# A two-layer decoder trunk: layer 0's heads in pairs, their buffers in the residual's place, and another order of its column groups

## The chip, the cores and the metric

The kernel runs on one core of a Trainium2 chip. The metric is device time in microseconds. Three runs of the kernel before took 2193.85, 2195.46 and 2195.37 us, median 2195.37.

## The reference

x is 256 tokens of 2048 features, float32. Layer 0 mixes by two recurrences that share one input projection; layer 1 by dilated attention. Each layer ends in a squared-ReLU MLP.

```
proj = rms_norm(x) @ w_in
x_lru, y_lru, q_h, f_h, v_h, g_h = split(proj)
# RG-LRU: conv of width 4, block-diagonal gates, scan
xb = causal_depthwise_conv(x_lru);  r, i = sigmoid(xb @ w_a + b_a), sigmoid(xb @ w_i + b_i)
h_t = a_t * h_(t-1) + sqrt(1 - a_t^2) * i_t * xb_t,   a = exp(-8 r softplus(-lambda))
lru = h * gelu(y_lru)
# HGRN2, per head of 128: S_t = diag(f_t) S_(t-1) + k_t v_t,  o_t = q_t S_t
q = silu(q_h);  f = lb + (1 - lb) sigmoid(f_h);  k = (1 - lb) sigmoid(-f_h)
hg = rms_norm_per_head(o) * g_norm * silu(g_h)
x = x + concat(lru, hg) @ w_out
x = x + relu(rms_norm(x) @ w1)^2 @ w2
# layer 1: qkv, partial rotary, attention over three dilated windows, w_o, MLP; then a final RMSNorm
```

## The kernel before

Weights come in units of 128 x 2048 (1 MB). SP's queue loads a unit into one of three `raw` buffers (L148); ACT rounds it to `hi` (L130) and DVE takes the difference `lo` (L131), again in three buffers each, so that the split of a unit can begin when the unit three before it has been used. `tokens` multiplies two blocks of 128 tokens by four units: 24 matmuls of 512 columns a unit (hi x hi, hi x lo, lo x hi; L221), into two of the three PSUM banks called `p`. `tokens_group` evicts the two banks on ACT into a tile `tk` (L360).

Layer 0's input projection runs through 12 groups of 512 columns in the order of `ORDER`: v, q, f and g are the four parts of HGRN2, x and y those of the RG-LRU, 0 and 1 their halves; G0 and G1 stand for the block-diagonal gates (`lru_gates`: 48 matmuls of 256 columns each). While a group's units run, `HOOKS` hands out other work, one list after each unit. A scheduler that simulates the engines decides the final order of each engine's instructions within that; the engines then run their instructions in this order.

The hooked work is:

- `hgrn(hd)`, one call a head: the head's columns of q and f are transposed on PE into the bank `pt` (`turned`, L436); sigmoids on ACT; the decayed scores are built from the diagonal (`pd`, L457) and eight levels c = 1, 2, 4 to 128. In a level PE multiplies into `pl` (L473), the result goes into `st` by a masked copy on DVE (L476) or by ACT copies (L481, L483), and DVE multiplies the factors of the next level into `qk` (L490) and shortens `tot` (L492). Level c = 128 is L468, L469. The next level's matmuls need the multiply. Then the output products into `po` (L497 to L499) and their squares on ACT (L504).
- `finish(g, half)`: for two heads, norm and gate on DVE (L518, L520), transposes into `pt`, and the split into `bufb` blocks 8 to 15 (L271, L272). It needs the column group g.
- `lru_in(n, half)`: transposes and convolution (L535, L537), split into `bufb` blocks 0 to 7 (L268, L269); `lru_gates(n)`; `lru_gelu(n)` (needs y); `lru_out(n, half)`: transposes of y, product with the scan (L579), split into the same blocks.

`bufb` then holds the 16 blocks that `out_project` multiplies by `w_out`: two column groups by `tokens`, with the residual add into `xres`, and two by `second`, in a form with fewer products, whose first bank is `po`. `xres` is the tile `xall` seen by tokens; it is loaded from `xtok` at the start (L367, L379) for the first norm, and added to only after `w_out`. In `w_out`'s first eight rows `PAIRED` puts blocks 0, 2, 4, 6 into one unit and 1, 3, 5, 7 into the next. The units of one column group come in the order 2, 3, 0, 1, so HGRN2's rows come first.

Of the kernel before, what the change touches and what calls it, by code (L numbers as in the profile page):

```python
# [10 lines left out]
F32 = mybir.dt.float32  # L11
# [4 lines left out]
AF = mybir.ActivationFunctionType  # L16
OP = mybir.AluOpType
# [3 lines left out]
P = 128  # L21
S = 256
# [19 lines left out]
def trunk_kernel(ctx, tc, head, x, xtok, cols, tab, masks, pos, fin, w_in, w_gate, w_out, w_qkv, w_o, w1, w2, out):  # L42
    nc = tc.nc
# [8 lines left out]
    pmm = pool("pmm", 3, space=PSUM)  # L52
    psc = pool("psc", 1, space=PSUM)
# [30 lines left out]
    units = []  # L84
# [12 lines left out]
    for g, step in enumerate(ORDER.split()):  # L97
        if step[0] == "G":
            units.append((w_gate, int(step[1])))
        else:  # L100
            units.extend((w_in, 4 * PLACE[step] + i) for i in range(4))
    units.extend((w_out, 4 * n + g) for n in range(2) for g in (2, 3, 0, 1))
    plan2(w_out, 8)
    for layer in range(2):
        if layer:
# [8 lines left out]
    at = [0, 0]  # L114
# [111 lines left out]
    later, turns, steps = [], [], []  # L226
# [24 lines left out]
    def lut(out_, in_, func, **kw):  # L251
        i = A.activation(out_, in_, func, **kw)
        if luts["kind"] != tables[func]:
            luts.update(kind=tables[func], before=luts["now"], now=[])
        luts["now"].append(after(i, luts["now"][:1] or luts["before"]))

    def direct(p, w, jobs):
        p = p[:, :S]
# [173 lines left out]
    def turned(tiles, at):  # L432
        p = psc.tile([P, 2, S], F32, name="pt", bufs=1)
        for i, (z, m) in enumerate(zip(tiles, at)):
            for j in range(2):
                T.transpose(p[:, i, j * P:j * P + P], z[:, j, m * P:m * P + P], ident)  # L436
        return p

    def halves(t, c, second):
        return t.rearrange("p (n two c) -> p n two c", two=2, c=c)[:, :, int(second), :]  # L440

    def hgrn(hd):
        g, at = divmod(hd, 4)
        oml = omlb[:, hd:hd + 1]
        qk = wk.tile([P, 2 * S], F32, name="qk", bufs=3)
        qp, kq = qk[:, :S], qk[:, S:]
        p = turned((done[f"q{g}"], done[f"f{g}"]), (at, at))
        lut(qp, p[:, 0], AF.Sigmoid)
        V.scalar_tensor_tensor(qp, p[:, 0], oml, qp, op0=OP.mult, op1=OP.mult)
        f = wk.tile([P, S], F32, name="f", bufs=3)  # L450
        lut(f, p[:, 1], AF.Sigmoid)
        lut(kq, p[:, 1], AF.Sigmoid, scale=-1.0)
        A.activation(f, f, AF.Identity, scale=oml, bias=lb[:, hd:hd + 1])
        pd = psc.tile([P, 2, P], F32, name="pd", bufs=1)
        for j in range(2):
            js = slice(j * P, j * P + P)
            T.matmul(pd[:, j], kq[:, js], qp[:, js], start=True, stop=True)  # L457
        st = wk.tile([P, 3, P], F32, name="st", bufs=3)
        V.tensor_tensor(st[:, :2], pd, ident[:, None, :].to_broadcast([P, 2, P]), OP.mult)
        stf = st[:, :2].rearrange("p a b -> p (a b)")  # L460
        V.tensor_tensor(qp, qp, f, OP.mult)
        c = 1
        tot = f
        while c <= 128:
            pl = psc.tile([P, 2, 64], F32, name="pl", bufs=2)
            if c == 128:
                plf = pl.rearrange("p j c -> p (j c)")
                T.matmul(plf, kq[:, :P], qp[:, P:], start=True, stop=True)  # L468
                A.copy(st[:, 2], plf)  # L469
                break  # L470
            for j in range(2):
                js = slice(j * P, j * P + P)
                T.matmul(pl[:, j], kq[:, js], halves(qp[:, js], c, True), start=True, stop=True)  # L473
            if c <= 16:
                lv = LEVELS.index(c)
                V.copy_predicated(halves(stf, c, True), msk[:, lv].rearrange("p (n c) -> p n c", c=c),  # L476
                                  pl.rearrange("p j (n c) -> p (j n) c", c=c))
            elif c == 32:
                for n in range(2):
                    ps_ = slice(64 * n, 64 * n + 32)  # L480
                    A.copy(st[ps_, :2, 64 * n + 32:64 * n + 64], pl[ps_, :, 32 * n:32 * n + 32])  # L481
            else:
                A.copy(st[:64, :2, 64:], pl[:64])  # L483
            n = S // (2 * c)
            tt = tot.rearrange("p (n two) -> p n two", two=2)
            both = bass.AP(tensor=qk.tensor, offset=qk.offset + c,
                           ap=[list(qk.ap[0]), [S - c, 2], [2 * c, n], [1, c]])
            fac = bass.AP(tensor=tot.tensor, offset=tot.offset,
                          ap=[list(tot.ap[0]), [1, 2], [2, n], [0, c]])
            V.tensor_tensor(both, both, fac, OP.mult)  # L490
            nt = wk.tile([P, n], F32, name=f"tot{n}", bufs=2)
            V.tensor_tensor(nt, tt[:, :, 0], tt[:, :, 1], OP.mult)  # L492
            tot = nt
            c *= 2
        vg, vs = done[f"v{g}"], slice(at * P, at * P + P)
        po = psc.tile([P, 2, P], F32, name="po", bufs=1)
        T.matmul(po[:, 0], st[:, 0], vg[:, 0, vs], start=True, stop=True)  # L497
        T.matmul(po[:, 1], st[:, 2], vg[:, 0, vs], start=True, stop=False)
        T.matmul(po[:, 1], st[:, 1], vg[:, 1, vs], start=False, stop=True)  # L499
        if not at:  # L500
            roots[g] = wk.tile([P, 8], F32, name="hs", bufs=2)
        o = outs[hd] = wk.tile([P, 2, P], F32, name="ho", bufs=6)
        for j in range(2):
            A.activation(o[:, j], po[:, j], AF.Square, accum_out=roots[g][:, 2 * at + j:2 * at + j + 1])  # L504
        A.copy(o, po)

    def finish(g, half):
# [33 lines left out]
    def lru_gates(gp):  # L541
        w = unit(w_gate, gp)
        room = act.tile([P, 8, S], F32, name="bufb3")
        gr, gi = room[:, :4], room[:, 4:]
        for m in range(4):
            b = 4 * gp + m
            for gate, (g, bname) in enumerate(((gr, "b_a"), (gi, "b_i"))):
                p = psc.tile([P, 512], F32, name="pl", bufs=2) if gp and not gate else pmm.tile([P, 512], F32, name="p")
                direct(p, w, [(gate * 8 + 2 * m + k, bufb[:, (b // 2) * 2 + k], k == 0, k == 1)
                              for k in range(2)])  # L550
                with urgent():
                    lut(g[:, m], p[:, :S], AF.Sigmoid, bias=col(bname, b))
# [22 lines left out]
    def lru_out(n, half):  # L575
# [4 lines left out]
        split_to(bufb[:, b0:b0 + 2], z)  # L580

    do = lambda f, *args: lambda: f(*args)
    head = lambda h: [do(hgrn, h)]
# [622 lines left out]
```

## Time and profile before

| | |
|---|---|
| median of three runs | 2195.37 us |
| profiled execution, its own time | 2196.22 us |
| its span | 2194.4 us |
| PE, DVE, ACT busy | 98%, 82%, 60% |
| mean granted PE clock | 0.986 |
| HBM read | 494.31 MB |

The span runs from the first to the last instruction; what lies around it is 1.8 us. PE busy counts a matmul for as long as it is in the array, also at a lower clock; the granted clock is listed beside it. In the trace a float32 product of the levels appears as two matmuls (224 at L473 for 112 in the program). The mixer of layer 0, with which the change deals, lies between the start and about 420 us. The lines of the profile are shown where they are used below.

### The profile page before, as it was taken

Reading aid. Unit: us, or ns where it says so; the run is one execution under the profiler, and the core shown is the slowest. Engines: PE = TensorE matmul, PEld = TensorE weight load, DVE = VectorE, ACT = ScalarE, POOL = GpSimd, SP = SyncE. Lnnn points to the kernel's source line nnn. Section 1 sums busy time; section 2 is a strip of 40 time slices with the busy share of each in tenths; the row PEclk is TensorE's granted clock in tenths of the full one; section 3 lists DMA queues with packets and bytes.
Section 4 is the critical chain, followed back from the end, with each engine's and each line's share of the span. In section 5 each row is a group of like instructions: output and inputs, shape, how many; then the busy total and the mean of one; then the engine's idle time right before and its main releaser. Section 6 shows DMA issues by size and latency. Waiting matters only on the chain.

```text
span 2194.4 us, 25011 instructions
## 1 busy us (share of the span) xinstructions
PE 2158.8 (98%) x9854; PEld 1784.0 (81%) x9854; DVE 1790.2 (82%) x1771; ACT 1312.4 (60%) x1337; POOL 72.5 (3%) x89
## 2 busy tenths in 40 slices
PE   9999988999999999999999999999999999999998
PEld 7888776788888888888887888888888888888887
DVE  6556847889879879888898888788988888888887
ACT  6445644566557557556666666656755755655664
POOL 0000000000000000000000000000000000000000
PEclk9999979999999999999999999999999999999999
DMA  8543414687787787788778767657778777877874
GB/s 334 187 161 136 169 46 146 197 260 233 238 275 238 246 254 247 248 250 267 235 230 260 234 208 228 217 161 252 252 238 260 255 244 238 268 239 244 268 261 154
DMA packets 69877, 498.03 MB, mean 227 GB/s; under 512 B 7808, under 2 KB 8064, under 8 KB 10240
## 3 DMA queue, kind: packets, MB, share of 16 engines
q1 hardware_dynamic: 57600, 410.90, 49.2%
q0 software_dynamic: 11872, 84.94, 20.6%
q8 instruction: 77, 1.26, 0.2%
q10 hardware_dynamic: 288, 0.61, 0.1%
q14 instruction: 40, 0.33, 0.0%
HBM read 494.31 MB, written 2.10 MB: 226 GB/s over the span
## 4 chain that ended last, share of the span: by engine, by line
PE 96%; DVE 2%; ACT 1%; DMA 1%; issue 0%; SPq 0%; DVEq 0%
PE p L221 60%; PE pd L221 14%; PE po L221 14%; PE pl L224 2%; PE pt L221 2%; PE pl L473 1%; PE pl L221 1%; DVE lo L131 1%; ACT hi L130 0%; PE pt L436 0%; DMA raw<-in_w_qkv 0%; DMA both_in<-in_head 0%; PE po L497 0%; DVE qk L490 0%; PE pd L457 0%
## 5 line engine op out<-in xcount | busy, mean ns | idle before, releaser
L131 DVE TENSOR_TENSOR lo<-raw,hi 128x2048 fp32r<-128x2048 f32 (+1 forms) x364 | 788.9, 2171 | 250.3 <-ACT hi L130 248.7
L130 ACT CAST hi<-raw 128x2048 fp32r<-128x2048 f32 (+1 forms) x364 | 659.1, 1816 | 531.1 <-PE p L221 329.0
L221 PE MATMUL p<-hi,bufa 128*128 128x512 f32 x2000 | 641.1, 393 | 0.8 <-ACT bufa L271 0.8
L221 PEld LDWEIGHTS p<-hi,bufa 128*128 128x128 f32 x2000 | 374.5, 188 | 78.6 <-ACT bufa L271 1.0
L221 PE MATMUL p<-hi,bufb 128*128 128x512 f32 x1264 | 409.7, 394 | 3.3 <-DVE bufb L269 2.2
L221 PE MATMUL p<-lo,bufa 128*128 128x512 f32 x1000 | 392.1, 392 | 1.3 <-DVE lo L131 1.3
L131 DVE TENSOR_TENSOR lo<-s,hi 128x2048 fp32r<-128x2048 f32 x120 | 274.2, 2285 | 12.7 <-ACT hi L130 10.6
L221 PEld LDWEIGHTS p<-hi,bufb 128*128 128x128 f32 x1264 | 238.7, 189 | 56.0 <-DVE bufb L269 3.1
L130 ACT CAST hi<-s 128x2048 fp32r<-128x2048 f32 x120 | 228.8, 1907 | 54.1 <-PE po L221 23.3
L221 PE MATMUL p<-lo,bufb 128*128 128x512 f32 x632 | 247.7, 392 | 0.0
L221 PEld LDWEIGHTS p<-lo,bufa 128*128 128x128 f32 x1000 | 187.9, 188 | 41.6 <-DVE lo L131 2.8
L221 PEld LDWEIGHTS p<-lo,bufb 128*128 128x128 f32 x632 | 119.6, 189 | 25.2
L221 PE MATMUL p<-hi,formx 128*128 128x512 f32 x352 | 118.3, 397 | 0.0
L221 PE MATMUL pd<-hi,bufa 128*128 128x512 f32 x352 | 116.7, 393 | 0.0
L131 DVE TENSOR_TENSOR lo<-t,hi 128x2048 fp32r<-128x2048 f32 x40 | 91.5, 2287 | 17.6 <-ACT hi L130 17.6
L221 PE MATMUL po<-hi,bufb 128*128 128x512 f32 (+1 forms) x320 | 102.3, 386 | 0.0
L221 PE MATMUL p<-hi,formh 128*128 128x512 f32 x288 | 96.3, 395 | 0.0
L159 DVE TENSOR_TENSOR s<-s,raw 128x2048 f32<-128x2048 f32 x40 | 91.3, 2283 | 2.9 <-DMA raw<-in_w_qkv 2.9
L159 DVE TENSOR_TENSOR s<-raw,t 128x2048 f32<-128x2048 f32 x40 | 91.3, 2283 | 0.4 <-DMA raw<-in_w_o 0.3
L221 PE MATMUL po<-hi,bufa 128*128 128x512 f32 x256 | 84.9, 392 | 0.0
L130 ACT CAST hi<-t 128x2048 fp32r<-128x2048 f32 x40 | 76.3, 1907 | 12.6 <-PE pd L221 6.4
L221 PE MATMUL pd<-hi,bufb 128*128 128x512 f32 x256 | 83.0, 389 | 0.0
(311 smaller groups left out, 2856.9 us busy)
## 6 DMA issues: line engine op xcount, KB each, us to landing
raw<-in_w SPq DMA_DIRECT2D x224, 1024.0 KB, 6.6
raw<-in_w_in SPq DMA_DIRECT2D x45, 1024.0 KB, 4.8
raw<-in_w_qkv SPq DMA_DIRECT2D x42, 1024.0 KB, 6.7
t<-in_w SPq DMA_DIRECT2D x32, 1024.0 KB, 6.8
t<-in_w POOLq DMA_DIRECT2D x32, 1024.0 KB, 8.5
s<-in_w POOLq DMA_DIRECT2D x32, 1024.0 KB, 8.7
raw<-in_w_out SPq DMA_DIRECT2D x15, 1024.0 KB, 4.8
raw<-in_w_o SPq DMA_DIRECT2D x15, 1024.0 KB, 4.9
```

The source lines that it names most:

```text
L130: casts[:] = [after(A.copy(h, w), [])]
L131: i = V.tensor_tensor(l, w, h.bitcast(F32), OP.subtract)
L159: return V.tensor_tensor(held[to], held[x], held[y], OP.add)
L221: chain[:] = [after(T.matmul(*args, **kw), chain)]
L224: chain[:] = [after(T.transpose(out_, in_, ident), chain)]
L473: T.matmul(pl[:, j], kq[:, js], halves(qp[:, js], c, True), start=True, stop=True)
```

## The change

`hgrn` takes a pair of heads. Each instruction on ACT and DVE covers both heads, as far as its per-head scalars allow; the PE products are the same as before. `qk`, `f` and the `tot` tiles no longer have tiles of their own: they lie in `xall`, the residual's tile, in two slots of 2048 elements, and `reload` brings x into `xres` again by two transfers of 1 MB. `st` has two buffers of two heads (before, three of one), `ho` four of two (before, six of one).

The column groups run in another order, in which q0 f0 x0 come before v1 q1 f1 x1, and g1 is last. `lru_gates` puts the two gates of a block into the halves of one `p` bank; before, half of G1's gates went to `pl`. In `out_project` the units come in the order 0, 1, 2, 3, so that the recurrence rows are first.

```diff
-    units.extend((w_out, 4 * n + g) for n in range(2) for g in (2, 3, 0, 1))
+    units.extend((w_out, 4 * n + g) for n in range(2) for g in range(4))
...
-    def hgrn(hd):
-        g, at = divmod(hd, 4)
...
-        qk = wk.tile([P, 2 * S], F32, name="qk", bufs=3)
-        qp, kq = qk[:, :S], qk[:, S:]
-        p = turned((done[f"q{g}"], done[f"f{g}"]), (at, at))
-        lut(qp, p[:, 0], AF.Sigmoid)
-        V.scalar_tensor_tensor(qp, p[:, 0], oml, qp, op0=OP.mult, op1=OP.mult)
+    def hgrn(c2):
+        g, at = c2 // 2, 2 * (c2 % 2)
+        heads = (2 * c2, 2 * c2 + 1)
+        slot = 2048 * (c2 % 2)
+        qk = xall[:, slot:slot + 1024].rearrange("p (t h s) -> p t h s", h=2, t=2)
+        qp, kq = qk[:, 0], qk[:, 1]
+        f = xall[:, slot + 1024:slot + 1536].rearrange("p (h s) -> p h s", h=2)
+        rest = [slot + 1536]
+        p = turned([done[f"q{g}"]] * 2, (at, at + 1))
+        lut(qp, p, AF.Sigmoid)
+        for h, hd in enumerate(heads):
+            V.scalar_tensor_tensor(qp[:, h], p[:, h], omlb[:, hd:hd + 1], qp[:, h], op0=OP.mult, op1=OP.mult)
+        p = turned([done[f"f{g}"]] * 2, (at, at + 1))
...
-            for j in range(2):
-                js = slice(j * P, j * P + P)
-                T.matmul(pl[:, j], kq[:, js], halves(qp[:, js], c, True), start=True, stop=True)
+            for h in range(2):
+                for j in range(2):
+                    js = slice(j * P, j * P + P)
+                    T.matmul(pl[:, h, j], kq[:, h, js], halves(qp[:, h, js], c, True), start=True, stop=True)
...
-            V.tensor_tensor(both, both, fac, OP.mult)
-            nt = wk.tile([P, n], F32, name=f"tot{n}", bufs=2)
-            V.tensor_tensor(nt, tt[:, :, 0], tt[:, :, 1], OP.mult)
+            V.tensor_tensor(both_, both_, fac, OP.mult)
+            nt = xall[:, rest[0]:rest[0] + 2 * n].rearrange("p (h n) -> p h n", h=2)
+            rest[0] += 2 * n
+            V.tensor_tensor(nt, tt[:, :, :, 0], tt[:, :, :, 1], OP.mult)
...
+            both_p = pmm.tile([P, 512], F32, name="p")
             for gate, (g, bname) in enumerate(((gr, "b_a"), (gi, "b_i"))):
-                p = psc.tile([P, 512], F32, name="pl", bufs=2) if gp and not gate else pmm.tile([P, 512], F32, name="p")
+                p = both_p[:, gate * S:gate * S + S]
...
+    def reload():
+        for j in range(2):
+            nc.sync.dma_start(xres[:, j], xtok[:, j])
...
-        "q1": [head(0)], "f1": [head(1)], "v1": [head(2)], "x0": [head(3)],
-        "x1": [head(4), [do(lru_in, 0, 0)], [do(lru_in, 0, 1)]],
-        "g0": [head(5), [do(lru_in, 1, 0)], [do(lru_in, 1, 1)]],
-        "g1": [head(6), [do(finish, 0, 0)], [do(finish, 0, 1)]],
-        "y0": [head(7)],
-        "y1": [[do(lru_gelu, 0)], [do(lru_out, 0, 0), do(lru_out, 0, 1)], [do(finish, 1, 0)], [do(finish, 1, 1)]],
+        "x0": [[do(hgrn, 0)], [], [do(hgrn, 1)]],
+        "q1": [[do(lru_in, 0, 0)], [], [do(lru_in, 0, 1)]],
+        "x1": [[do(hgrn, 2)], [], [do(hgrn, 3)]],
+        "y0": [[], [do(lru_in, 1, 0)], [], [do(lru_in, 1, 1)]],
+        "y1": [[do(lru_gelu, 0)], [do(finish, 0, 0)], [do(lru_out, 0, 0)], [do(lru_out, 0, 1), do(finish, 0, 1)]],
+        "g1": [[do(lru_gelu, 1)], [do(reload)], [do(lru_out, 1, 0)], [do(lru_out, 1, 1)]],
...
-    steps[:] = [[do(lru_gelu, 1)], [do(lru_out, 1, 0), do(lru_out, 1, 1), close_mixers]]
+    steps[:] = [[do(finish, 1, 0), do(finish, 1, 1)], [close_mixers]]
...
-    nrm = out_project(w_out, "nmlp0", (2, 3, 0, 1))
+    nrm = out_project(w_out, "nmlp0", (0, 1, 2, 3))
...
-ORDER = "v0 q0 f0 q1 f1 v1 x0 x1 G0 g0 g1 G1 y0 y1"
+ORDER = "v0 q0 f0 x0 v1 q1 f1 x1 G0 y0 g0 G1 y1 g1"
```

More of the change, by code (lines that the diff above doesn't have):

```diff
@@ L257, in direct @@
     def direct(p, w, jobs):
-        p = p[:, :S]
         for blk, mov, first, last in jobs:
@@ L440, in halves @@
         return t.rearrange("p (n two c) -> p n two c", two=2, c=c)[:, :, int(second), :]
-    def hgrn(hd):
-        g, at = divmod(hd, 4)
-        oml = omlb[:, hd:hd + 1]
-        qk = wk.tile([P, 2 * S], F32, name="qk", bufs=3)
-        qp, kq = qk[:, :S], qk[:, S:]
-        p = turned((done[f"q{g}"], done[f"f{g}"]), (at, at))
-        lut(qp, p[:, 0], AF.Sigmoid)
-        V.scalar_tensor_tensor(qp, p[:, 0], oml, qp, op0=OP.mult, op1=OP.mult)
[L450 to L454, printed above, removed]
-        for j in range(2):
-            js = slice(j * P, j * P + P)
[L457 to L460, printed above, removed]
+    def hgrn(c2):
[11 more added lines that the diff above has]
+        p = turned([done[f"f{g}"]] * 2, (at, at + 1))
+        lut(f, p, AF.Sigmoid)
+        lut(kq, p, AF.Sigmoid, scale=-1.0)
+        for h, hd in enumerate(heads):
+            A.activation(f[:, h], f[:, h], AF.Identity, scale=omlb[:, hd:hd + 1], bias=lb[:, hd:hd + 1])
+        pd = psc.tile([P, 2, 2, P], F32, name="pd", bufs=1)
+        for h in range(2):
+            for j in range(2):
+                js = slice(j * P, j * P + P)
+                T.matmul(pd[:, h, j], kq[:, h, js], qp[:, h, js], start=True, stop=True)
+        st = wk.tile([P, 2, 3, P], F32, name="st", bufs=2)
+        V.tensor_tensor(st[:, :, :2], pd, ident[:, None, None, :].to_broadcast([P, 2, 2, P]), OP.mult)
+        stf = st[:, :, :2].rearrange("p h a b -> p h (a b)")
@@ L464, in hgrn @@
         while c <= 128:
-            pl = psc.tile([P, 2, 64], F32, name="pl", bufs=2)
+            pl = psc.tile([P, 2, 2, 64], F32, name="pl", bufs=2)
             if c == 128:
-                plf = pl.rearrange("p j c -> p (j c)")
-                T.matmul(plf, kq[:, :P], qp[:, P:], start=True, stop=True)
-                A.copy(st[:, 2], plf)
+                plf = pl.rearrange("p h j c -> p h (j c)")
+                for h in range(2):
+                    T.matmul(plf[:, h], kq[:, h, :P], qp[:, h, P:], start=True, stop=True)
+                A.copy(st[:, :, 2], plf)
                 break
-            for j in range(2):
-                js = slice(j * P, j * P + P)
-                T.matmul(pl[:, j], kq[:, js], halves(qp[:, js], c, True), start=True, stop=True)
+            for h in range(2):
+                for j in range(2):
+                    js = slice(j * P, j * P + P)
+                    T.matmul(pl[:, h, j], kq[:, h, js], halves(qp[:, h, js], c, True), start=True, stop=True)
             if c <= 16:
                 lv = LEVELS.index(c)
-                V.copy_predicated(halves(stf, c, True), msk[:, lv].rearrange("p (n c) -> p n c", c=c),
-                                  pl.rearrange("p j (n c) -> p (j n) c", c=c))
+                V.copy_predicated(stf.rearrange("p h (n two c) -> p h n two c", two=2, c=c)[:, :, :, 1],
+                                  msk[:, lv].rearrange("p (n c) -> p n c", c=c)[:, None].to_broadcast([P, 2, P // c, c]),
+                                  pl.rearrange("p h j (n c) -> p h (j n) c", c=c))
             elif c == 32:
@@ L480, in hgrn @@
                     ps_ = slice(64 * n, 64 * n + 32)
-                    A.copy(st[ps_, :2, 64 * n + 32:64 * n + 64], pl[ps_, :, 32 * n:32 * n + 32])
+                    A.copy(st[ps_, :, :2, 64 * n + 32:64 * n + 64], pl[ps_, :, :, 32 * n:32 * n + 32])
             else:
-                A.copy(st[:64, :2, 64:], pl[:64])
+                A.copy(st[:64, :, :2, 64:], pl[:64])
             n = S // (2 * c)
-            tt = tot.rearrange("p (n two) -> p n two", two=2)
-            both = bass.AP(tensor=qk.tensor, offset=qk.offset + c,
-                           ap=[list(qk.ap[0]), [S - c, 2], [2 * c, n], [1, c]])
+            tt = tot.rearrange("p h (n two) -> p h n two", two=2)
@@ L488, in hgrn @@
+            both_ = bass.AP(tensor=qk.tensor, offset=qk.offset + c,
+                            ap=[list(qk.ap[0]), [2 * S - c, 2], [2 * c, 2 * n], [1, c]])
             fac = bass.AP(tensor=tot.tensor, offset=tot.offset,
-                          ap=[list(tot.ap[0]), [1, 2], [2, n], [0, c]])
-            V.tensor_tensor(both, both, fac, OP.mult)
-            nt = wk.tile([P, n], F32, name=f"tot{n}", bufs=2)
-            V.tensor_tensor(nt, tt[:, :, 0], tt[:, :, 1], OP.mult)
+                          ap=[list(tot.ap[0]), [1, 2], [2, 2 * n], [0, c]])
@@ L493, in hgrn @@
+            V.tensor_tensor(both_, both_, fac, OP.mult)
+            nt = xall[:, rest[0]:rest[0] + 2 * n].rearrange("p (h n) -> p h n", h=2)
+            rest[0] += 2 * n
+            V.tensor_tensor(nt, tt[:, :, :, 0], tt[:, :, :, 1], OP.mult)
             tot = nt
             c *= 2
[L495 to L498, printed above, removed]
@@ L499, in hgrn @@
-        T.matmul(po[:, 1], st[:, 1], vg[:, 1, vs], start=False, stop=True)
+        vg = done[f"v{g}"]
+        po = psc.tile([P, 2, 2, P], F32, name="po", bufs=1)
+        for h in range(2):
+            vs = slice((at + h) * P, (at + h) * P + P)
+            T.matmul(po[:, h, 0], st[:, h, 0], vg[:, 0, vs], start=True, stop=True)
+            T.matmul(po[:, h, 1], st[:, h, 2], vg[:, 0, vs], start=True, stop=False)
+            T.matmul(po[:, h, 1], st[:, h, 1], vg[:, 1, vs], start=False, stop=True)
@@ L500, in hgrn @@
         if not at:
             roots[g] = wk.tile([P, 8], F32, name="hs", bufs=2)
-        o = outs[hd] = wk.tile([P, 2, P], F32, name="ho", bufs=6)
-        for j in range(2):
-            A.activation(o[:, j], po[:, j], AF.Square, accum_out=roots[g][:, 2 * at + j:2 * at + j + 1])
+        o = wk.tile([P, 2, 2, P], F32, name="ho", bufs=4)
+        for h in range(2):
+            for j in range(2):
+                n = 2 * (at + h) + j
+                A.activation(o[:, h, j], po[:, h, j], AF.Square, accum_out=roots[g][:, n:n + 1])
+            outs[heads[h]] = o[:, h]
@@ L551, in lru_gates @@
                 with urgent():
-                    lut(g[:, m], p[:, :S], AF.Sigmoid, bias=col(bname, b))
+                    lut(g[:, m], p, AF.Sigmoid, bias=col(bname, b))
         for m in range(4):
@@ L582, in trunk_kernel @@
     do = lambda f, *args: lambda: f(*args)
-    head = lambda h: [do(hgrn, h)]
+    def reload():
+        for j in range(2):
+            nc.sync.dma_start(xres[:, j], xtok[:, j])
     HOOKS.update({
-        "q1": [head(0)], "f1": [head(1)], "v1": [head(2)], "x0": [head(3)],
-        "x1": [head(4), [do(lru_in, 0, 0)], [do(lru_in, 0, 1)]],
-        "g0": [head(5), [do(lru_in, 1, 0)], [do(lru_in, 1, 1)]],
-        "g1": [head(6), [do(finish, 0, 0)], [do(finish, 0, 1)]],
-        "y0": [head(7)],
-        "y1": [[do(lru_gelu, 0)], [do(lru_out, 0, 0), do(lru_out, 0, 1)], [do(finish, 1, 0)], [do(finish, 1, 1)]],
+        "x0": [[do(hgrn, 0)], [], [do(hgrn, 1)]],
[4 more added lines that the diff above has]
+        "g1": [[do(lru_gelu, 1)], [do(reload)], [do(lru_out, 1, 0)], [do(lru_out, 1, 1)]],
     })
```

## The prediction

> **What bounds the kernel now.** I began with the page of the profile (span, busy shares, slices), then cut the first 500 us into windows and looked for stretches in which TensorE (PE) has work but does not run it densely.
>
> ```profile
> span 2194.4 us, 25011 instructions
> PE 2158.8 (98%) x9854; PEld 1784.0 (81%) x9854; DVE 1790.2 (82%) x1771; ACT 1312.4 (60%) x1337; POOL 72.5 (3%) x89
> PEclk9999979999999999999999999999999999999999
> ```
>
> PE is busy for 98% of the span, so nothing else can be the bound over the whole; but "busy" includes matmuls at a lower clock, and the only slice with a clock digit under 9 is the sixth, 274 to 329 us. That is in layer 0's mixer, the stage the change rewrites.
>
> ```profile
> core 0: us, PE busy (x) PEld busy (x) DVE busy (x) ACT busy (x) POOL busy (x), PEclk, DMA share, GB/s
> 100.00:190.00 90.00, 90.00 (x451) 75.90 (x451) 50.46 (x79) 40.69 (x57) 0.00 (x0) 1.00 0.48 171
> 197.40:213.00 15.60, 13.20 (x86) 12.54 (x86) 10.80 (x28) 8.29 (x21) 0.00 (x0) 0.78 0.32 124
> 264.00:308.70 44.70, 31.68 (x150) 29.10 (x149) 16.34 (x45) 12.76 (x39) 0.00 (x0) 0.58 0.11 44
> 361.40:390.70 29.30, 20.52 (x78) 14.86 (x77) 19.58 (x50) 10.82 (x23) 0.00 (x0) 0.77 0.36 132
> 400.00:500.00 100.00, 100.00 (x459) 82.42 (x458) 87.17 (x83) 64.76 (x71) 4.44 (x5) 1.00 0.73 231
> ```
>
> Three windows stand out: around the first gate step G0 (granted clock 0.78), around the second, G1 (0.58), and at the entry to the output projection (0.77). Outside them, 100 to 190 and 400 to 500 us, PE is full at clock 1.00. I call the three holes. What each could have cost at most needs the dense price of a matmul, which the chain of waits gives:
>
> ```profile
> 277.05 1.10 PE pl L473 x4
> 278.46 0.34 DVE qk L490
> 278.94 1.10 PE pl L473 x4
> 305.92 0.72 PE pl L221 x6
> 419.91 2.72 PE po L221 x12
> ...
> 448.44 0.87 PE pl L224 x8
> 452.05 5.44 PE po L221 x24
> ```
>
> A wide matmul (512 columns) costs 5.44/24 = 0.227 us, a gate matmul (256 columns) 0.72/6 = 0.12, a small one (a transpose, or a pass of a 64 or 128 column product) 0.87/8 = 0.109. The first three rows show one level of one head with nothing else on PE: 1.89 us per level, for four small matmuls worth 0.44.
>
> ```profile
> 197.40:213.00 15.60, 6.91 (x48) 6.12 (x49) 0.78 0.32 124
> 264.00:308.70 44.70, 8.21 (x50) 7.86 (x50) 0.58 0.11 44
> 361.40:390.70 29.30, 15.65 (x46) 10.34 (x46) 0.77 0.36 132
> ```
>
> These are the same windows for L221 alone. G0: 48 gate matmuls and 86 - 48 = 38 small ones, 5.8 + 4.1 = 9.9 us dense, against 15.6: 5.7 lost. G1: 48 gates, 2 wide, 100 small, 5.8 + 0.5 + 10.9 = 17.1 against 44.7: 27.6 lost. Entry to the projection: 46 wide, 32 small, 10.4 + 3.5 = 13.9 against 29.3: 15.4 lost. Together **48.7 us** that PE could give back; no change that leaves its work alone gives more here.
>
> **The change part by part.** *PE's work stays.* Two heads per call issue the same products, transposes and gates as two calls; only their order moves. In the built programs the PE instructions from the output projection's first product on po onwards are identical, as are DVE's and ACT's a little later, so all gains and losses lie before about 420 us.
>
> *Levels go from single heads to pairs.* What a level costs off PE:
>
> ```profile
> L131 DVE TENSOR_TENSOR lo<-raw,hi 128x2048 fp32r<-128x2048 f32 (+1 forms) x55 | 106.2, 1940 | 71.7 <-ACT hi L130 71.7
> L490 DVE TENSOR_TENSOR qk<-qk,tot 128x256 f32<-128x256 f32 x48 | 20.4, 425 | 5.3 <-PE pl L473 5.3
> L476 DVE COPY_PREDICATED st<-msk,pl 128x128 f32<-128x128 int8 x40 | 14.1, 352 | 18.6 <-PE pl L473 18.6
> L579 DVE TENSOR_TENSOR tk<-pt,xc 128x512 f32<-128x512 f32 x4 | 2.7, 687 | 4.4 <-PE pt L436 4.4
> L520 DVE SCALAR_TENSOR_TENSOR ho<-ho,hr,g 128x128 f32<-128x128 f32 x16 | 4.7, 346 | 0.1
> L537 DVE SCALAR_TENSOR_TENSOR xc<-pt,c__91,xc 128x253 f32<-128x253 f32 (+2 forms) x24 | 11.5, 479 | 1.9 <-ACT xc L535 1.6
> L518 DVE TENSOR_TENSOR g<-g,tk 128x256 f32<-128x256 f32 x8 | 3.1, 419 | 0.0
> L272 DVE SCALAR_TENSOR_TENSOR bufb<-pt,c__91,bufb 128x256 fp32r<-128x256 f32 x8 | 3.8, 481 | 4.0 <-ACT bufb L271 4.0
> ```
>
> The paired multiply has 512 elements a lane: 0.69 us by the 512 wide L579, in place of 2 x 0.425. The paired masked copy has no row: it lies between 0.35 (L476 as it is) and 0.70 (twice that); I take 0.55. A paired level is then about 0.55 + 0.69 = 1.24 on DVE for two heads. In the built order, outside the gate steps, the four pairs run one after the other, one level per weight unit: eight small matmuls, then 21 to 32 wide ones, typically 24 (5.44 us). Behind the products DVE may first have one weight difference to do (2.29 us in the chain below), so the next level's input is ready after at most 2.29 + 1.24 = 3.5 us, well inside 5.44. I cost the 20-odd such levels at nothing; the cover is those 24 matmuls, and without it each costs about 1.9 like the bare levels above.
>
> *G1 loses its bare levels.* Before, 17 groups of L473 stand there almost without wide work between them. In the new order only the last two levels of the last pair fall at G1, and gates stand around what follows. Between those two products there is only the multiply: 0.69 and two hand-overs of about 0.1 make 0.9 us. Bounds: 0 if the clock and order are kind, 5 if the clock drops as well. I take **0.9**.
>
> *G0 gets the third pair's first four levels.* The order there is six gates, level 1, four transposes, level 2, 12 gates, next pair's diagonal, transposes, 12 gates, level 4, 12 gates, level 8, six gates, then wide work. Level 1 to 2: copy and multiply (1.24) and hand-overs (0.2) against four transposes (0.44): 1.0 us stall. Level 4 to 8: its copy is queued on DVE behind about 4 us of the fourth pair's setup and the convolution (two 0.69, several 0.42 to 0.48), so its products wait about 1.4 us beyond the gates that cover them. The stalls sum to 2.4. A clock drop may follow:
>
> ```profile
> 197.43 1.80 ACT hi L130
> 199.26 2.29 DVE lo L131
> 202.62 1.04 PE pl L473 x4
> 361.62 0.93 issue
> 380.40 1.06 ACT hi L130
> 381.48 2.36 DVE lo L131 x2
> ```
>
> In the old G0 a level was late behind a cast and a weight difference, PE stood about 1.7 us before 202.62, and from there four small matmuls took 1.04, not 0.44: the clock had halved (0.78 for the window). The 0.93 us at 361.62 brought no drop at once. New stalls of 1.0 and 1.4 lie between: 0 to 3.4 us (half of the 6.8 that 15.6 x 0.22 x 2 gives for the low clock in the old window). I take the middle, 1.7, so G0 costs **4.1** (1 to 8).
> [...]
>
> *The entry to the projection.* w_out now starts with the recurrence rows, and g1 is the last column group, so finish(1, ...) must wait for it. Call T the end of g1. The first unit needs blocks 0, 2, 4, 6 of bufb. PE's new order is three wide, four transposes, three wide, eight transposes of lru_out(1, ...), three wide, four transposes, three wide. All transposes share one bank, pt, so each group of four waits until the one before it was read.
>
> ```profile
> L360 ACT ACTIVATE tk<-p,nr 128x512 f32<-128x512 f32 x20 | 13.7, 687 | 24.6 <-PE p L221 24.6
> L252 ACT ACTIVATE bufb<-p,c__91 128x256 f32<-128x256 f32 x12 | 5.4, 473 | 2.4 <-PE p L221 2.4
> L268 ACT CAST bufb<-tk 128x512 fp32r<-128x512 f32 x4 | 2.5, 613 | 4.1 <-DVE tk L579 4.1
> L269 DVE TENSOR_TENSOR bufb<-tk,bufb 128x512 fp32r<-128x512 f32 x4 | 2.7, 686 | 0.7 <-ACT bufb L268 0.7
> ```
>
> On ACT there stand after T one eviction (0.7) and the third w_out unit's cast, whose buffer g1's last unit frees (1.06 per half); on DVE that unit's difference (2.36 in two halves, ending about T + 4.5), then two L518 (0.8), L272 (0.48), four L520 (1.2), L272: pt is free at about **T + 7.4**. PE has done its first work by T + 2 and stands 5.4 us. Then transposes, L518 and L520 of the next half (2.0), L579 (0.69), L268 and L269 (0.6 and 0.7): the third three start at T + 11.4; the fourth, behind the second L579 and four more transposes, end near T + 14.9 at half clock. Dense, these 12 wide and 16 small are 4.5, so 10.4 lost, and 1.6 more until the clock is back: **12**. Bounds: 6 if DVE has the third unit done earlier or takes finish sooner, 17 if two more turns of pt come serially. The old entry lost 15.4.
>
> *Reload.* Two 1 MB transfers of x into xall, since the head buffers overwrite it. They stand on SP's queue between the loads of y1 and g1; the first waits for pair 3's products, long done, the second for pair 4's at G1.
>
> ```profile
> raw<-in_w_in SPq DMA_DIRECT2D x45, 1024.0 KB, 4.8
> ```
>
> Each takes about 4.8 us, while the DMA share here is 0.11 to 0.48 and three raw buffers run ahead: nothing. Were that cover gone it would be up to 9.6. The gates now use one p bank per pair of gates instead of alternating with pl; two sigmoids per bank (2 x 0.473) against 12 gate matmuls (1.44 us) cost nothing.
>
> *Sum.* Old losses 48.7; new 0.9 + 4.1 + 12 = 17.0; gain 31.7. The profiled execution took 2196.22 us (span 2194.4): 2164.5. It lies 0.85 above the median of the runs, 2195.37, so I forecast **2164 us**.
>
> **The rivals.** *The waits move into the gate steps.* If pairing makes DVE late throughout G0 and G1, both run at the clock 0.58 of the old G1: their 96 gates and about 84 small matmuls (52 at G0, 32 at G1; 11.5 + 9.2 = 20.7 dense) would take 20.7/0.58 = 35.7, 15 lost instead of 5: 2174. For it, the DVE backlog at G0; against, gates stand between almost all levels. *The entry hides.* If ACT and DVE reach the finish work early, losses there fall to 6 and the clock holds at G0: 2156. For it, DVE is only 56% busy at 100 to 190; against, g1 is needed. *Slower:* a paired level does not fit into one unit. If a cast (1.80), the difference (2.29), three convolution steps (3 x 0.479) and the level (1.24, and 0.2) always queue in series, it is 6.9 us against 5.44, 1.5 for each of 28 levels, 42 more: 2206. It decides from about 1.1 us of wait per level (31.7/28). Against it: cast and difference run a unit ahead, and the old stage of single heads ran full at clock 1.00 at 100 to 190. *No effect:* the holes come from the gate path, not the levels, and return: 2195; against it, the waits name the level multiply:
>
> ```profile
> PE pl L473 <- DVE qk L490: 11.7, 14, 1.5
> ```
>
> **How the numbers follow.** Forecast 0.66, waits in the gate steps 0.14, entry hidden 0.12, slower 0.05, no effect 0.03. The forecast's own bounds (0 to 5, 1 to 8, 6 to 17) give losses of 7 to 30, 2154 to 2177, with 2156 and 2174 of the two faster rivals inside; since the dense prices are good to some 10% of the 48.7 only, I add 4 to 5 on either side: **2150 to 2182**. A measurement tells about 0.2% (4.4 us): all three faster cases are beyond it, 0.92; within it 0.03; slower 0.05.
>
> **What would show it.** Right: the first po product of the projection starts near 388 us (419.91 - 31.7); no window of bare L473-like groups; G1 at clock 0.9 or more; one idle stretch of about 5 us after g1 ended by a pt transpose waiting for DVE or ACT, and clock under 1 only there and perhaps at G0. Wrong: PE waiting for the paired multiply in every unit; SP or DMA as releaser of a weight cast; a long wait at the first reading of bufb's block 0.

## The result, and the profile after

The changed kernel takes 2162.41 us (median of four runs, 2161.77 to 2163.06) against 2195.41 us for the kernel before (four runs, 2193.85 to 2196.13): ratio 0.9851, 95% interval 0.9834 to 0.9868. The forecast was 2164 us.

The page of the changed kernel (span 2160.7 us), its row of busy times and its clock row:

```profile
PE 2140.7 (99%) x9854; PEld 1771.6 (82%) x9854; DVE 1781.6 (82%) x1687; ACT 1307.5 (61%) x1305; POOL 72.4 (3%) x89
PEclk9999999999999999999999999999999999999999
```

The clock digit under 9 is gone. PE has as many instructions as before, DVE 84 fewer, ACT 32 fewer. The new places of the three holes, as windows (columns as in the prediction), first with every engine and then with L221 alone (matmuls, weight loads, clock, DMA share, GB/s):

```profile
205.40:217.90 12.50, 11.58 (x98) 11.15 (x97) 11.13 (x27) 8.64 (x15) 0.00 (x0) 1.00 0.31 109
271.00:284.10 13.10, 11.15 (x77) 10.36 (x76) 5.09 (x7) 8.17 (x14) 0.00 (x0) 0.87 0.53 188
329.60:349.40 19.80, 13.69 (x55) 10.71 (x54) 12.47 (x25) 9.36 (x16) 0.00 (x0) 0.74 0.25 99
```

```profile
205.40:217.90 12.50, 6.76 (x50) 6.02 (x49) 1.00 0.31 109
271.00:284.10 13.10, 7.46 (x45) 6.54 (x44) 0.87 0.53 188
329.60:349.40 19.80, 11.09 (x37) 7.67 (x35) 0.74 0.25 99
```

With the prediction's dense prices (0.227 us for a wide matmul, 0.12 for a gate, 0.109 for a small one): G0 has 48 gates, 2 wide and 48 small matmuls, 11.4 us, so 1.1 of its 12.5 are lost. G1 has 48 gates (of which a few are missing from the trace) and 32 small, 9.3 us, so 3.8 are lost. The entry has 37 wide and 18 small, 10.4 us, so 9.4 are lost.

| lost, us | before | forecast | after |
|---|---|---|---|
| G0 | 5.7 | 4.1 | 1.1 |
| G1 | 27.6 | 0.9 | 3.8 |
| entry to the projection | 15.4 | 12 | 9.4 |
| sum | 48.7 | 17.0 | 14.3 |

Between the holes the paired levels stand on the chain of waits, each with its wide matmuls directly behind it and nothing between:

```profile
222.79 0.84 PE pl L480 x8
223.63 5.74 PE p L221 x25
229.37 0.84 PE pl L480 x8
230.21 6.00 PE p L221 x26
```

The entry, on the same chain:

```profile
331.56 2.36 DVE lo L131 x2
333.92 0.67 DVE g L532 x2
334.59 0.40 DVE bufb L271
334.99 1.05 DVE ho L534 x4
...
338.15 0.61 DVE tk L594
...
338.80 1.11 PE pt L435 x4
339.92 1.28 PE p L221 x3
...
386.16 2.72 PE po L221 x12
```

This is the serial piece that the prediction described: the third unit's difference, then `finish` and `lru_out` in turn on DVE, and the transposes on PE waiting for them. When the next three wide matmuls run, the clock is halved (1.28 us, dense 0.68; 0.50 granted from 334.1 to 344.4). PE's own timeline there, with the idle time ahead of an entry in brackets:

```profile
331.21 0.40 PE L221 MATMUL p<-hi,bufb 128*128 128x512 f32 x1
336.58 1.09 PE L435 MATMUL pt<-tab__183,tk 128*128 128x128 f32 x4 [4.97 <-DVE bufb L271]
...
339.57 0.78 PE L221 MATMUL p<-hi,bufb 128*128 128x512 f32 x1
```

Behind the wide matmul that starts at 331.21, PE stands idle for 4.97 us, until the transposes of 336.58.

The chain's last row shown is the first product on `po`: it starts at 386.16; it was 419.91. The 33.75 us between them are the gain of the one profiled execution over the other (2196.22 - 2162.48); by the medians it is 33.0. Behind this product nothing changes. That holds for all kernels below: the profiled execution's time minus the start of this product is 1776.0 to 1776.7 us in each, so its start tells each kernel's gain.

TensorE's waits before 430 us, by what ended them (total, times, longest):

```profile
PE pt L435 <- DVE bufb L271: 5.0, 1, 5.0
PE pl L480 <- DVE xall L498: 1.7, 2, 0.9
...
PE p L221 <- ACT bufb L252: 0.9, 1, 0.9
```

The level multiply, which was waited for 14 times and 11.7 us, is left with two waits. The last row, the gates waiting for a bank, the forecast had put at nothing.

### The profile page after: what moved, and what is told of

It is laid out like the page before. It is cut to its first block, busy times and chain, and to the rows that moved or that the text cites. A ratio compares the mean times of both kernels' runs of the same rounds, so it can differ in the third digit from the quotient of the medians.

```text
span 2160.7 us, 24875 instructions
## 1 busy us (share of the span) xinstructions
PE 2140.7 (99%) x9854; PEld 1771.6 (82%) x9854; DVE 1781.6 (82%) x1687; ACT 1307.5 (61%) x1305; POOL 72.4 (3%) x89
## 4 chain that ended last, share of the span: by engine, by line
PE 97%; DVE 1%; DMA 1%; ACT 0%; issue 0%; DVEq 0%
PE p L221 62%; PE pd L221 14%; PE po L221 14%; PE pl L224 2%; PE pt L221 2%; PE pl L480 1%; PE pl L221 1%; DVE lo L131 0%; DMA raw<-in_w_qkv 0%; PE pt L435 0%; DMA both_in<-in_head 0%; ACT hi L130 0%; PE pd L462 0%; DVE s L159 0%; DVE ho L534 0%
## 5 line engine op out<-in xcount | busy, mean ns | idle before, releaser
L221 PE MATMUL p<-hi,bufa 128*128 128x512 f32 x2000 | 641.1, 393 | 0.6 <-ACT bufa L270 0.6
L221 PEld LDWEIGHTS p<-hi,bufa 128*128 128x128 f32 x2000 | 375.7, 188 | 79.0 <-ACT bufa L270 0.9
L221 PE MATMUL p<-hi,bufb 128*128 128x512 f32 x1264 | 407.9, 393 | 0.0
L221 PE MATMUL p<-lo,bufa 128*128 128x512 f32 x1000 | 392.1, 392 | 1.1 <-DVE lo L131 1.1
L221 PEld LDWEIGHTS p<-hi,bufb 128*128 128x128 f32 x1264 | 238.3, 189 | 50.5
L221 PE MATMUL p<-lo,bufb 128*128 128x512 f32 x632 | 247.0, 391 | 0.0
L221 PEld LDWEIGHTS p<-lo,bufa 128*128 128x128 f32 x1000 | 188.3, 188 | 40.6 <-DVE lo L131 1.6
L221 PEld LDWEIGHTS p<-lo,bufb 128*128 128x128 f32 x632 | 119.2, 189 | 25.1
L221 PE MATMUL p<-hi,formx 128*128 128x512 f32 x352 | 118.3, 397 | 0.0
L221 PE MATMUL pd<-hi,bufa 128*128 128x512 f32 x352 | 116.7, 393 | 0.0
L221 PE MATMUL po<-hi,bufb 128*128 128x512 f32 (+1 forms) x320 | 102.3, 386 | 0.0
L221 PE MATMUL p<-hi,formh 128*128 128x512 f32 x288 | 96.3, 395 | 0.0
L221 PE MATMUL po<-hi,bufa 128*128 128x512 f32 x256 | 84.9, 392 | 0.0
L221 PE MATMUL pd<-hi,bufb 128*128 128x512 f32 x256 | 83.0, 389 | 0.0
```

The lines of the kernel that those rows point to most:

```text
L221: chain[:] = [after(T.matmul(*args, **kw), chain)]
```

## The experiments

### What pairing is worth, and what the order is worth

**One head a call in the new order.** The changed kernel with `hgrn(hd)` for one head, called twice at each place; buffers still in the residual's tile, a slot of 1024 each.

```diff
-        "x0": [[do(hgrn, 0)], [], [do(hgrn, 1)]],
+        "x0": [[do(hgrn, 0), do(hgrn, 1)], [], [do(hgrn, 2), do(hgrn, 3)]],
...
-        "x1": [[do(hgrn, 2)], [], [do(hgrn, 3)]],
+        "x1": [[do(hgrn, 4), do(hgrn, 5)], [], [do(hgrn, 6), do(hgrn, 7)]],
```

> The changed kernel with one head per call again (buffers still in xall, two calls where one pair was). Theory (a level step is paced by the weight units, about one per 24 wide matmuls, so pairing halves the steps from 56 to 28): the last heads' levels run over into y1, g1 and the projection; some 10 bare levels of 1.9 us and a later entry, 2185 us (2175 to 2200). Rival (the order of the column groups alone makes the gain): 2162, within 4.

Measured: 2176.93 us (2175.03 to 2177.23), ratio 0.9914 (0.99 to 0.9929): the rival is out, and the time lies in the theory's range, but 8 us under its 2185. Its waits between 190 and 402 us, and its window around G1 (every engine, then L221 alone):

```profile
PE pl L474 <- DVE xall L491: 3.9, 5, 0.9
...
PE pl L474 <- DVE xall L494: 2.8, 1, 2.8
PE pl L474 <- DVE rs L324: 1.6, 1, 1.6
```

```profile
258.00:285.00 27.00, 21.04 (x119) 18.82 (x118) 21.34 (x52) 15.53 (x30) 0.00 (x0) 0.81 0.34 117
258.00:285.00 27.00, 14.31 (x75) 11.80 (x75) 0.81 0.34 117
```

In these rows levels (L474) wait for DVE seven times, 8.3 us in all, and the granted clock is 0.81 from 258 to 285 us and 0.80 from 350 to 385. Levels run until 359.3, when products of `w_out` have long begun (one stands at 339.9), so they do run over into the projection. At G1 there are 48 gates, 27 wide and 44 small matmuls, 16.7 us by the dense prices, so about 10 of the 27 us are lost. The first product on `po` starts at 400.43. So in the new order pairing is worth 14.5 us (2176.93 - 2162.41).

**Pairs in the old order.** The changed kernel with the old column order and the old order of `w_out`'s units.

```diff
-ORDER = "v0 q0 f0 x0 v1 q1 f1 x1 G0 y0 g0 G1 y1 g1"
+ORDER = "v0 q0 f0 q1 f1 v1 x0 x1 G0 g0 g1 G1 y0 y1"
...
+        "q1": [[do(hgrn, 0)]], "v1": [[do(hgrn, 1)]],
+        "x1": [[do(hgrn, 2)], [do(lru_in, 0, 0)], [do(lru_in, 0, 1)]],
+        "g0": [[], [do(lru_in, 1, 0)], [do(lru_in, 1, 1)]],
+        "g1": [[do(hgrn, 3)], [do(finish, 0, 0)], [do(finish, 0, 1)]],
+        "y1": [[do(lru_gelu, 0), do(reload)], [do(lru_out, 0, 0), do(lru_out, 0, 1)], [do(finish, 1, 0)], [do(finish, 1, 1)]],
```

> Pairs, but the old order of column groups and of w_out's rows, the third pair hooked at x1 and the fourth at g1. Theory (pairing is what removes the bare levels at G1): G1 holds three levels of the last pair with gates between, G0 three or four nearly bare ones of the second pair, so 15 to 25 of the 33 us gain stay: 2175 (2168 to 2182). Rival (the new order is what does it): 2190 to 2196.

Measured: 2166.09 us (2165.95 to 2166.36), ratio 0.9867 (0.9852 to 0.9882). Theory and rival both missed. The windows around G0, G1 and the entry:

```profile
205.50:218.00 12.50, 9.05 (x43) 8.49 (x44) 11.18 (x28) 4.88 (x8) 0.00 (x0) 0.64 0.24 84
272.00:284.30 12.30, 10.79 (x90) 10.28 (x90) 10.88 (x24) 7.26 (x13) 0.00 (x0) 1.00 0.48 172
338.50:360.00 21.50, 16.00 (x64) 11.51 (x63) 13.66 (x26) 7.65 (x12) 0.00 (x0) 0.92 0.45 154
```

At G1, the hole of 27.6 us before, 90 matmuls (50 of them L221: 48 gates and 2 wide) now run at clock 1.00 in 12.3 us, and 1.7 are lost: pairing closes it without the new order. That fits the theory, by which 28 level steps find room between the units where 56 did not. What the old order keeps is a loss at G0, where a level's copy (L483) and multiply (L498) stand on DVE behind a weight difference that ends at 209.10 (clock 0.64; 18 gates and 25 small matmuls, 4.9 us dense, so 7.6 of the 12.5 are lost). At the entry 52 wide and 12 small, 13.1 us, leave 8.4 of the 21.5 lost.

The four corners: neither 2195.4, new order with single heads 2176.9 (18.5 us), pairs in the old order 2166.1 (29.3 us), both 2162.4 (33.0 us). The gains do not add up, because both close the same hole: G1 loses 27.6 us with neither, about 10 with the order, 1.7 with the pairs and 3.8 with both. Pairing carries most of it. The buffers in the residual's tile and the gates on one bank are part of all three new corners; no run shows what they do by themselves.

### The order of w_out's rows

**Recurrence rows first in the kernel before.**

```diff
-    nrm = out_project(w_out, "nmlp0", (2, 3, 0, 1))
+    nrm = out_project(w_out, "nmlp0", (0, 1, 2, 3))
```

and the units of `w_out` in the same order. The first such unit is handed out before `lru_out(1, ...)`, so it reads blocks 4 and 6 of `bufb` as `lru_in` left them: the projection is of other data, and there is no wait for the late rows.

> The kernel before with only w_out's row order changed. Theory (the row order gives nothing where y1 comes last, since its blocks 4 and 6 are the last to be ready): 2195 to 2203. Rival (recurrence rows first is a gain of its own): under 2190.

Measured: 2194.77 us (2191.95 to 2195.86), ratio 0.9997 (0.9988 to 1.0006). Without the wait this says nothing about the theory. So the next one calls the late steps first:

```diff
-    steps[:] = [[do(lru_gelu, 1)], [do(lru_out, 1, 0), do(lru_out, 1, 1), close_mixers]]
+    lru_gelu(1)
+    for half in range(2):
+        lru_out(1, half)
+    steps[:] = [[], [close_mixers]]
```

> The kernel before with w_out's units in the order 0,1,2,3 (recurrence rows first), nothing else of the change; lru_gelu(1) and both lru_out(1) steps are called ahead of the projection so that its first units read what they write. The same work is done. Theory: in the old column order the recurrence rows are the late ones, so the new order of w_out's units makes the projection wait for them from its first unit: 2195 to 2203 us. Rival: the order of w_out's units by itself is worth time, whatever is finished when: below 2190 us.

Measured: 2198.29 us (2197.13 to 2199.02), ratio 1.0013 (1.0004 to 1.0023): within the theory's range, and the rival is out. Its windows around G1 and the entry:

```profile
264.00:308.70 44.70, 31.67 (x158) 28.86 (x157) 16.32 (x45) 14.82 (x42) 0.00 (x0) 0.66 0.11 40
354.00:392.00 38.00, 26.66 (x104) 19.62 (x103) 27.27 (x66) 15.12 (x30) 0.00 (x0) 0.73 0.27 91
```

The first product on `po` starts 0.9 us later than before, at 420.77, although G1 ran at clock 0.66, not 0.58. By the dense prices (59 of the 158 matmuls and 68 of the 104 are L221) G1 lost 25.6 us, 2.0 less than before, and the entry 18.6, 3.2 more. The range held the old time as well, and the edit also moves `lru_gelu` and `lru_out` ahead, so the run excludes a gain from the order of the rows here, but does not show what the wait for the late rows alone costs.

**Old rows first in the changed kernel.** The reverse of the same edit, units in the order 2, 3, 0, 1.

> The changed kernel with w_out's rows in the old order (HGRN2's first). Theory (the 5.4 us stall after g1 comes from needing lru_out(1, ...) in the first unit while pt waits for DVE): the first unit needs finish(0, 1) only and the second finish(1, ...), so the entry loses 3 to 7 instead of 9.7: 2158 (2155 to 2162). Rival (recurrence rows first is a gain with g1 last): 2166 to 2172.

Measured: 2164.39 us (2162.67 to 2165.23), ratio 0.9857 (0.984 to 0.9873). The forecast of a gain was wrong; the rival's range was missed as well, and the difference from the changed kernel, 2.0 us, is not beyond the intervals, which overlap. The long idle is gone, but:

```profile
329.60:333.00 3.40, 1.39 (x7) 0.66 (x5) 2.76 (x4) 2.54 (x5) 0.00 (x0) 1.00 0.25 106
333.00:339.80 6.80, 6.08 (x16) 4.59 (x17) 5.12 (x15) 1.92 (x4) 0.00 (x0) 0.50 0.41 154
...
346.70:353.50 6.80, 6.66 (x17) 4.52 (x17) 5.18 (x15) 2.09 (x4) 0.00 (x0) 0.50 0.70 265
```

Twice the clock is at 0.50 for 6.8 us, behind shorter stalls: TensorE's waits from 320 to 360 us are five, 5.4 us in all, the longest 1.9. `finish(1, ...)` and `lru_out(1, ...)` both come late here, so neither order of the rows spares the entry.

### What makes the entry's idle

**Banks of its own for lru_out(1, ...).** Nothing but the bank of these eight transposes is edited; the order of the instructions follows from it.

```diff
-    def turned(tiles, at):
-        p = psc.tile([P, 2, S], F32, name="pt", bufs=1)
+    def turned(tiles, at, bank="pt"):
+        p = psc.tile([P, 2, S], F32, name=bank, bufs=1)
...
-        p = turned([done[f"y{n}"]] * 2, (2 * half, 2 * half + 1))
+        p = turned([done[f"y{n}"]] * 2, (2 * half, 2 * half + 1), ("pd", "po")[half] if n else "pt")
```

> The changed kernel, with the transposes of lru_out(1, 0) and lru_out(1, 1) in the PSUM banks pd and po, which no level uses any more, and not in the one bank pt that finish(0, 1) and finish(1, 0) also use. The same work is done. In the changed kernel TensorE stands idle for 5.4 us (331.21 to 336.58) because the next product in its order is a transpose into pt, and pt has to be read and written in turn by lru_out(1, 0), lru_out(1, 1), finish(0, 1). Theory: the turn-taking on the one bank is what makes these 5.4 us; with banks of their own the two lru_out steps run early, the entry's loss falls from 9.7 us to 2 to 5 us, and the time is 2155 to 2159 us. Rival: the limit is VectorE, which has the work of both lru_out steps and of three finish steps to do in the same microseconds whatever the bank; then the idle only moves by a few units of 6 matmuls and the time is 2161 to 2164 us.

Measured: 2157.3 us (2156.17 to 2157.93), ratio 0.9828 (0.9811 to 0.9844), as the theory said; no run is as slow as the fastest of the changed kernel. The same stretch on its chain:

```profile
330.56 2.36 DVE lo L131 x2
332.92 0.67 DVE g L532 x2
333.59 0.61 DVE bufb L268
...
334.25 5.75 PE p L221 x24
```

DVE's difference, 2.36 us, stands about where it stood (1 us earlier), but the `lru_out` products now lie ahead of it, and 24 wide matmuls follow at 334.25 where the changed kernel's PE was waiting for its second turn of `pt`. With banks of their own the transposes of `lru_out(1, ...)` also stand earlier in PE's order: they run from 322.33 and 328.70, in the changed kernel from 336.58 and 338.80. The clock stays up:

```profile
329.00:354.00 25.00, 21.89 (x100) 16.88 (x99) 20.14 (x40) 14.13 (x22) 0.00 (x0) 1.00 0.52 196
```

85 of these 100 matmuls are wide, 20.9 us dense with the rest, so the entry loses 4.1 us and not 9.4; the difference, 5.3, is about the gain of 5.1. The idle was thus made by the turns on one PSUM bank, and by the order that they force, not by DVE's amount of work, which is the same.

**The sigmoid's table loaded ahead of G1, in addition.** ACT's timeline at G1 in the changed kernel (start, duration):

```profile
271.23 0.69 ACT L359 ACTIVATE tk<-p,nr 128x512 f32<-128x512 f32 x1 [1.90 <-PE p L221]
271.82 1.89 ACT L130 CAST hi<-raw 128x2048 fp32r<-128x2048 f32 x1
273.72 1.28 ACT L252 ACT_TABLE_LOAD   x1
275.02 0.47 ACT L252 ACTIVATE bufb<-p,c__91 128x256 f32<-128x256 f32 x1
```

The gates' first sigmoid stands behind an eviction, a cast and a table load, and PE waits 0.9 us for the bank that it frees. A sigmoid of one column behind the first unit of g0 moves the load:

```diff
+        "g0": [[do(lut, spare, epsc, AF.Sigmoid)]],
```

> As the run before it, and a dummy sigmoid of one column is put on ScalarE in the first step of the y0 group's successor g0, ahead of G1, so that ScalarE holds the sigmoid's table before the gates' first eviction. The same work is done otherwise. In the changed kernel a table load of 1.28 us (273.72 to 275.0) stands ahead of G1's second eviction, TensorE waits 0.9 us for a bank, and the clock is down from 276.1 to 279.5. Theory: without the load G1 loses 1 us rather than 4.3 and the clock stays up; the time is 2 to 3.5 us under that of the run before it. Rival: the load is needed again anyway (another function is called between), or the wait is made by the copies queued ahead, not by the load: within 1 us of the run before it.

Measured: 2154.76 us (2154.21 to 2156.22), ratio 0.9816 (0.9801 to 0.9831), by the medians 2.5 us under the run before it; the slowest run of the one (2156.22) and the fastest of the other (2156.17) just touch. On ACT, the load is gone from G1 (it now stands at 229.28), and the sigmoid follows the cast:

```profile
271.14 1.89 ACT L130 CAST hi<-raw 128x2048 fp32r<-128x2048 f32 x1
272.93 0.48 ACT L252 ACTIVATE bufb<-p,c__91 128x256 f32<-128x256 f32 x1
```

PE's wait for the bank falls from 0.9 to 0.3 us, and no stretch of the profiled execution before 430 us shows a lowered clock. That may not hold for each execution: two of the four runs have a mean granted clock of 0.998, the profiled one 0.999. This version beats both kernels: 7.6 us less than the changed one, and its slowest run is under the fastest of that one. It is 40.6 us under the kernel before (2195.32 in the same runs), of which 33.0 are the change's.

### The reload

Three reloads instead of one: six transfers of 1 MB, 4 MB more.

```diff
-        for j in range(2):
-            nc.sync.dma_start(xres[:, j], xtok[:, j])
+        for _ in range(3):
+            for j in range(2):
+                nc.sync.dma_start(xres[:, j], xtok[:, j])
```

> The changed kernel with the reload of the residual done three times over, six transfers and not two (4 MB more to read; same result). The prediction put the reload at nothing: its two transfers are issued behind other work and end long before the projection's residual is added. Theory: two more reloads are hidden too: 2160 to 2164.5 us. Rival: the transfers delay the weights that are streamed for the last groups, so that each reload shows: 2167 us or more.

Measured: 2161.44 us (2159.48 to 2162.62), ratio 0.9845 (0.983 to 0.9859): the transfers are hidden. Its trace has eight transfers from `xtok`, two at the start and the six.

## Why the prediction was right, point by point

**The bound and the place.** Right. PE's instructions are as many as before, and all of the gain lies ahead of the first product on `po`: forecast near 388, measured 386.16. That the time came out within 2 us is in part luck: G0 was put 3.0 us too high, G1 2.9 too low, and the two cancel; what is left of the difference is the entry, put 2.6 too high.

**The paired level's price.** Right. Rows of the changed kernel, grouped by line:

```profile
L498 DVE TENSOR_TENSOR xall<-xall 128x512 f32<-128x512 f32 x28 | 19.5, 696 | 1.6 <-PE pl L480 1.6
L483 DVE COPY_PREDICATED st<-msk,pl 128x256 f32<-128x256 int8 x20 | 11.0, 550 | 7.2 <-PE pl L480 6.9
```

The multiply takes 0.696 us (0.69 was taken), the masked copy 0.550, the value taken between 0.35 and 0.70. That levels outside the gates cost nothing holds: the chain shows 25 and 26 wide matmuls behind two of them and no wait, and the level multiply's two waits both lie at the gates.

**G1, 0.9 us.** The bare levels went as described, but the size was wrong: 3.8, within the bound of 5, and the window's clock is 0.87, where 0.9 or more was named as a sign of being right. The one wait between the last two levels is there (0.8 us; with the one at G0 it makes the 1.7 of the row). The rest comes from the step that the gates on one bank cost nothing. It counted two sigmoids against twelve matmuls, but not what stands ahead of the first on ACT, the cast of 1.89 and the table load of 1.28. PE's wait for the bank (0.9), and a clock drop of 3.4 us behind the two waits (0.50 from 276.1 to 279.5, 1.7 lost), make up most of the 3.0 that remain. The last experiment moves the load away, and the median falls by 2.5 us.

**G0, 4.1 us.** Mis-sized: 1.1. The stall behind level 1 came (0.9 us); that behind level 4 was to be 1.4, and no such wait is among PE's. The two gaps from which a clock drop was estimated were misread: PE's idle ahead of 202.62 is 1.54 us, not 1.7, and the 0.93 at 361.62 is a piece of the chain, in which PE idles 0.52. The 1.7 us for that drop did not come; the window's clock is 1.00. The two stalls alone, which the prediction summed to 2.4, would have come nearer.

**The entry, 12 us.** The right mechanism, and somewhat less: 9.4. T, the end of g1, is 329.6. PE's idle is 4.97 us (forecast 5.4); `pt` is free at T + 7.0 (forecast T + 7.4), and the third three matmuls start at T + 10.0 (T + 11.4). The forecast added the rows' durations, but in the trace the rows of neighbours on DVE lie partly over each other: the two products that were L518 still last 0.418 us each, but 0.75 together (333.84, the next row starts at 334.51), and take 0.67 in the chain, not 0.8, the four that were L520 1.05, not 1.2. That the shared bank is the cause, which the prediction argued, the run with banks of their own shows.

**Reload.** At nothing: right by the run with three.

**The rivals.** "The entry hides" (2156) came half true: the clock held at G0, but the entry lost 9.4 and not 6. That the run with separate banks arrives near its time, 2157.3, has another reason, the banks. "The waits move into the gate steps" (2174), "slower" (2206) and "no effect" are out: the level multiply has two waits left, 1.7 us.

**My expectations of the runs.** Two fell. For pairs in the old order I gave the order too much of the gain; for the old rows in the changed kernel I took it that the entry's idle was made by the rows' order.

## What to carry to other kernels

When a chain of short products waits for another engine at every step, count the steps against the units of independent work that they can be put between; halving the steps, by giving each instruction two heads, can be worth more than a better order (here 29.3 us by itself against 18.5). Where groups of transposes come late together, look at how often they take turns on one PSUM bank before looking at the engines that read it (banks of their own were worth 5.1 us here). Ahead of a burst that needs an activation function, look at what ScalarE has queued, a table load among it (here 1.28 us).

## What the runs showed of the clock

Where the clock fell in the stretches below, it stood at 0.50, for 3.4 us (the changed kernel at G1), 6.8 us (the kernel before at G0) or 10.3 us (the changed kernel at the entry). The 3.4 us ahead of such a drop and the drop itself, first in the kernel before:

```profile
199.29:202.70 3.41, 1.87 (x15) 1.59 (x15) 3.41 (x5) 1.97 (x5) 0.00 (x0) 1.00 0.17 48
202.70:209.50 6.80, 5.94 (x27) 5.56 (x27) 4.90 (x16) 2.17 (x7) 0.00 (x0) 0.50 0.39 151
```

then in the changed kernel, G0 without a drop, G1 and the entry each with one:

```profile
207.90:211.30 3.40, 2.81 (x24) 2.82 (x25) 3.40 (x5) 3.15 (x8) 0.00 (x0) 1.00 0.00 0
...
272.69:276.10 3.41, 1.72 (x13) 1.52 (x13) 3.06 (x3) 3.34 (x6) 0.00 (x0) 1.00 0.17 70
276.10:279.50 3.40, 3.26 (x16) 2.97 (x15) 0.96 (x2) 1.14 (x3) 0.00 (x0) 0.50 0.63 217
330.70:334.10 3.40, 0.90 (x5) 0.42 (x3) 2.57 (x4) 2.76 (x5) 0.00 (x0) 1.00 0.35 147
334.10:344.40 10.30, 6.68 (x21) 5.27 (x22) 7.60 (x20) 3.49 (x7) 0.00 (x0) 0.50 0.28 102
```

and in the last version, at the entry, without one:

```profile
329.00:332.40 3.40, 1.93 (x8) 0.92 (x6) 3.40 (x5) 2.34 (x5) 0.00 (x0) 1.00 0.07 19
```

In the run with separate banks PE is busy for 2.03 us of the 3.40 from 271.70, with a drop behind it (0.50 from 275.10 to 278.50). PE's busy time alone does not tell these stretches apart: a drop stands behind 0.90, 1.72, 1.87 and 2.03 us, and none behind 1.93 and 2.81.

At G0 of the changed kernel a single stall of 0.9 us cost only itself. At G1 two such stalls (0.78 us ahead of 273.53, 0.91 ahead of 275.55) stand close together, a drop follows them, and it cost a further 1.7 us (half of 3.4). The run with three reloads has waits of the same length (two for the level multiply, 1.7 us in all, and up to 0.9 for the gates' bank), but around G1 its clock stays at 1.00:

```profile
265.00:292.00 27.00, 24.84 (x150) 21.78 (x149) 14.80 (x30) 20.74 (x39) 0.00 (x0) 1.00 0.57 203
```

So the 1.7 us need not be part of each execution. What sets off a drop was not tested by itself, and no run shows it.
